# One core, two transformer blocks in float32: order of the products in a step, first squares, forget logits, key sums and norm sums

## The chip, the core and the metric

The kernel runs on one of the eight cores of a Trainium2 chip. A core has TensorE for matrix products (PE, its weight loads are listed as PEld), VectorE (DVE), ScalarE (ACT), GpSimd (POOL) and SyncE (SP), which mainly issues transfers; all work side by side and wait for each other by semaphores. TensorE reads SBUF and adds up in PSUM. The metric is the device time of one execution in microseconds (us). A profile records one execution; its span runs from the first to the last instruction.

## The reference

Two blocks follow each other on x, 256 positions of 2048 channels, all in float32. The first has four branches, the second three, then both have an MLP:

```python
xn = rms_norm(x, norm_mix_g); proj = xn @ w_in          # LRU, pool, short conv, attention, gates
f_logit = proj[..., forget columns]                      # 8 of them, one per head
cum = cumsum(log_sigmoid(f_logit + f_bias))              # enters the first attention's logits
x = x + sum_k(sigmoid(gate_k) * (y_k @ w_branch_k)) @ w_out
x = x + square(relu(rms_norm(x) @ w_mlp_up)) @ w_mlp_down
# second block: gMLP, state-space mixer (s5), stick-breaking attention
z = q @ k.T * scale
log_1m = where(mask, log_sigmoid(-z), 0)
after = cumsum(log_1m, reverse) - log_1m                 # the key sums
w = where(mask, exp(log_sigmoid(z) + after), 0); y = w @ v
return rms_norm(x, final_g)                              # after the second block's own MLP
```

A norm needs the mean of squares over all 2048 channels of a position.

## The kernel before, in words

**Layout.** x stands transposed: `T4[0..3]` are four tiles of 128 channels-in-partitions x 4 x 256 positions. The big products run on float32r, which TensorE takes in one pass, where a float32 product shows up as two passes in the profile. To keep precision, every operand is split in a high part and a rest (`split`, `split_scaled`): ScalarE writes the high part as float32r, VectorE subtracts it and writes the rest. `R[0..7]` hold split activations, high and low side by side, so 512 columns; x itself goes to `xg` = `R[0..3]` multiplied by the norm's gain `gs`, while the norm's factor per position is multiplied in when a product leaves PSUM.

**Steps.** The weights come in units of 1 MB (two steps). The list of products is a list of groups, each of four to eight steps that add up in one of two PSUM buffers `ps`. For each step, ScalarE casts its weights' high part (L145) and VectorE takes the rest (L76, `w<-raw,w`), three steps ahead (`AHEAD`), into one of four buffers `w`; the raw unit's buffer is then free for a later load. In mode "F" (L166 to L170) the weights stay in TensorE and x moves: per step two halves m of the output rows times four k, each a product of the high weights with 512 columns (high and low x) and one of the low weights with 256 columns (high x). In mode "W" the activations stay and the weights move, twelve products of 512 columns.

**Order.** One loop over the steps (`run_stream`) writes everything: it splits the weights of step i + 3, lets finished groups leave PSUM (`late`), writes the products of step i, and then spends a budget of VectorE time on two chains of small work (`chain_a`, `chain_b`: norms, branches, attention, state scan). A chain's `yield None` means: go on in the next step. `need` runs chain_a on at once until a flag is set, where a group depends on it. `hold` keeps a group in PSUM until the norm's factor is there.

**The start.** `first_work` issues the first loads on SP: x's first quarter, the gains, the first unit in two parts, x's second quarter, the second unit, and so on. Steps 0 to 3 also split one quarter of x each (`split_x`), and `squares_x` lets GpSimd square it and add it up in `acc`. `norm` then sums over the channels by products with a column of ones: eight passes of one column on TensorE (x4 in the program, each float32 product two passes), then GpSimd takes the power -0.5, and two products spread the factor over the partitions.

**Forget logits** (`forget`): sixteen products of `wfr` (the eight columns, high and low side by side, 16 wide) with the split x, 512 columns each; then four small products with `sel` add high and low and turn the result.

**Second attention** (`attn2`): per half two rounds of two heads; `e` holds the terms per key, and products with the triangle `tri` and with ones give the sums over keys, in float32 (names `mx<-e,k` and `mx<-e,cst`), six per round. "bu" and "yps" are chain_b's small products: "bu" is a pair of 256 columns on float32r, "yps" eight float32 products into four groups of 32 output rows.

**The end.** The last norm ("n5") sums `acc` and `sq2`, the square of the last group, twelve passes behind the final square; then the output is multiplied by the factor and stored.

## Time and profile before

| | |
|---|---|
| median of 3 runs | 3056.75 us (3053.06 to 3058.41) |
| profiled execution | 3056.62 us, its span 3054.4 us |
| mean granted clock of TensorE | 0.996 of full speed |
| TensorE busy | 3021.8 us (99%), 16127 products (passes counted) |
| weight loads busy | 2576.8 us (84%) |
| VectorE busy | 2061.9 us (68%) |
| ScalarE busy | 1406.2 us (46%) |
| GpSimd busy | 87.9 us (3%) |
| transfers | 604 MB, mean 198 GB/s |

The busy time of a product reaches from its start to its modelled end, so products that follow each other overlap, and the pace is read from starts and counts, not from the busy time. A row of the time order merges like instructions that follow each other; its first number is the start of the first. Names: `w<-raw,w` is the split of weights, `ps<-R,w` a product of mode F, `ps<-w,R` one of mode W, `mx` a small PSUM tile. In a row of a stretch, the counts hold every instruction that touches it, those that reach in from before too.

### The profile page before, as it was taken

Reading aid. Unit: us, or ns where it says so; the run is one execution under the profiler, and the core shown is the slowest. Engines: PE = TensorE matmul, PEld = TensorE weight load, DVE = VectorE, ACT = ScalarE, POOL = GpSimd, SP = SyncE. Lnnn points to the kernel's source line nnn. Section 1 sums busy time; section 2 is a strip of 40 time slices with the busy share of each in tenths; the row PEclk is TensorE's granted clock in tenths of the full one; section 3 lists DMA queues with packets and bytes.
Section 4 is the critical chain, followed back from the end, with each engine's and each line's share of the span. In section 5 each row is a group of like instructions: output and inputs, shape, how many; then the busy total and the mean of one; then the engine's idle time right before and its main releaser. Section 6 shows DMA issues by size and latency. Waiting matters only on the chain.

```text
span 3054.4 us, 39707 instructions
## 1 busy us (share of the span) xinstructions
PE 3021.8 (99%) x16127; PEld 2576.8 (84%) x16127; DVE 2061.9 (68%) x2524; ACT 1406.2 (46%) x1657; POOL 87.9 (3%) x115
## 2 busy tenths in 40 slices
PE   7999999999999999999999999999999999999998
PEld 6888888888888888888888887888888888888887
DVE  6765555556788976566678889966666656565565
ACT  4455544444444434344445564455444434344443
POOL 3000000000000000000010100000000000000000
PEclk9999999999999999999999999999999999999999
DMA  5544455555566665555576666765655555555553
GB/s 211 179 179 163 169 193 193 193 212 188 194 227 215 227 215 199 187 186 193 203 255 215 200 230 219 245 211 199 210 202 184 183 190 183 189 183 189 184 189 124
DMA packets 162071, 603.97 MB, mean 198 GB/s; under 512 B 11568, under 2 KB 13920, under 8 KB 161632
## 3 DMA queue, kind: packets, MB, share of 16 engines
q1 hardware_dynamic: 150528, 569.96, 52.8%
q0 software_dynamic: 7328, 24.12, 2.8%
q10 hardware_dynamic: 4032, 7.34, 0.9%
q8 instruction: 127, 2.08, 0.3%
q14 instruction: 56, 0.46, 0.0%
HBM read 583.53 MB, written 17.85 MB: 197 GB/s over the span
## 4 chain that ended last, share of the span: by engine, by line
PE 74%; issue 24%; DVE 1%; DMA 0%; ACT 0%; SPq 0%; POOLq 0%; POOL 0%; DVEq 0%; ACTq 0%
PE ps L91 72%; PE mx L91 2%; DVE w L76 0%; DVE R L85 0%; PE bu L91 0%; DMA T<-in_x 0%; PE yps L91 0%; PE mx L448 0%; DVE T L76 0%; ACT w L145 0%; PE mx L992 0%; DVE pa L76 0%; PE mx L1115 0%; DVE acc L76 0%; DVE sg L85 0%
## 5 line engine op out<-in xcount | busy, mean ns | idle before, releaser
L91 PE MATMUL ps<-R,w 128*128 128x512 f32 (+1 forms) x11264 | 2002.3, 340 | 17.1 <-ACT w L145 8.8
L91 PEld LDWEIGHTS ps<-R,w 128*128 128x128 f32 x11264 | 1729.7, 189 | 280.4 <-DVE w L76 9.2
L76 DVE TENSOR_TENSOR w<-raw,w 128x1024 fp32r<-128x1024 f32 x1048 | 1282.2, 1224 | 947.0 <-ACT w L145 944.9
L145 ACT CAST w<-raw 128x1024 fp32r<-128x1024 f32 x1048 | 1101.2, 1051 | 1545.3 <-PE ps L91 1375.6
L91 PE MATMUL ps<-w,R 128*128 128x512 f32 x4128 | 951.9, 391 | 0.0
L91 PEld LDWEIGHTS ps<-w,R 128*128 128x128 f32 x4128 | 771.8, 188 | 160.9 <-issue 1.8
L76 DVE TENSOR_TENSOR T<-T,ps 128x512 f32<-128x512 f32 x160 | 109.3, 683 | 9.1 <-PE ps L91 6.3
L76 DVE TENSOR_TENSOR ab<-ps,ab 128x512 f32<-128x512 f32 x98 | 66.9, 683 | 0.0
L332 POOL TENSOR_TENSOR rt<-nv,mh 128x2 f32<-128x2 f32 x5 | 3.5, 706 | 2011.0 <-DVE nv L82 2011.0
L378 ACT COPY ab<-ps 128x512 f32<-128x512 f32 x98 | 56.8, 579 | 0.0
L76 DVE TENSOR_TENSOR R<-ab,R 128x512 fp32r<-128x512 f32 x68 | 46.6, 685 | 0.0
L76 DVE TENSOR_TENSOR ab<-ab,rbc 128x512 f32<-128x512 f32 x64 | 44.3, 692 | 2.2
L96 ACT CAST R<-ab 128x512 fp32r<-128x512 f32 x68 | 41.8, 615 | 5.6 <-DVE ab L76 5.4
L85 DVE SCALAR_TENSOR_TENSOR ab<-ab 128x512 f32<-128x512 f32 x64 | 43.8, 684 | 0.0
L85 DVE SCALAR_TENSOR_TENSOR R<-T,gs,R 128x256 fp32r<-128x256 f32 x64 | 39.1, 657 | 4.3 <-ACT R L88 4.3
L1398 DVE TENSOR_TENSOR_SCAN pb<-magT,pa 128x256 f32<-128x256 f32 x64 | 40.7, 676 | 0.7
L88 ACT ACT_TABLE_LOAD x28 | 35.9, 1283 | 1.2 <-PEq L1528 0.7
L88 ACT ACTIVATE R<-T,gs 128x256 fp32r<-128x256 f32 x64 | 28.5, 498 | 4.9 <-DMA T<-in_x 2.7
L1341 POOL DMA_DIRECT2D tab<-dtab x32 | 17.8, 557 | 248.0 <-DVE pz L76 181.0
L76 DVE TENSOR_TENSOR sg<-ps,sg 128x1024 f32<-128x1024 f32 (+1 forms) x24 | 22.8, 952 | 2.4 <-PE ps L91 2.4
L76 DVE TENSOR_TENSOR pa<-pa,pb 128x256 f32<-128x256 f32 x64 | 24.1, 417 | 0.1
L76 DVE TENSOR_TENSOR T<-T,sg 128x1024 f32<-128x1024 f32 (+1 forms) x24 | 23.0, 958 | 0.8
(229 smaller groups left out, 862.3 us busy)
## 6 DMA issues: line engine op xcount, KB each, us to landing
raw<-in_w_in SPq DMA_DIRECT2D x191, 1024.0 KB, 4.7
raw<-in_w_up SPq DMA_DIRECT2D x128, 1024.0 KB, 4.8
raw<-in_w_down SPq DMA_DIRECT2D x128, 1024.0 KB, 4.8
raw<-in_w_branch SPq DMA_DIRECT2D x40, 1024.0 KB, 4.9
raw<-in_w_out SPq DMA_DIRECT2D x32, 1024.0 KB, 4.7
dtab<-tb SPq DMA_DIRECT2D x16, 512.0 KB, 7.5
tab<-dtab POOLq DMA_DIRECT2D x32, 256.0 KB, 3.9
sg<-dbg ACTq DMA_DIRECT2D x20, 256.0 KB, 4.7
```

The source lines that it names most:

```text
L76: self.V.tensor_tensor(out, a, b, op=op)
L85: self.V.scalar_tensor_tensor(out, a, s, b, op0=op0, op1=op1)
L88: self.A.activation(out, a, func, **kw)
L91: self.T.matmul(out, lhsT, rhs, start=start, stop=stop, skip_group_check=True)
L96: self.A.copy(hi, src)
L145: self.A.copy(hi, raw)
L332: self.G.tensor_tensor(out, v, self.mh[:, 0:out.shape[-1]], op=ALU.pow)
L378: self.A.copy(t, ps[:, :, 1])
L1341: self.G.dma_start(tab[t], self.d_tab[t // 2][:, t % 2])
L1398: self.V.tensor_tensor_scan(b[:, c], mg, a[:, c], 0.0, op0=MUL, op1=ADD)
```

## The change

1. In mode F a step now writes its eight products of 512 columns first and then its eight of 256 (`mm_step`).
2. The start: gains on ScalarE's queue, x's first quarter and the first unit's first step in two parts each, x's second quarter ahead of the first unit's second step; step 0's weights are split in two halves; five float32 products on zeros stand ahead of the first step.
3. The squares of x are taken by ScalarE behind the casts of steps 4 and 5, two each, and VectorE adds them (`sum_squares_x`).
4. `norm` adds the two halves of `acc` on VectorE first (`fold_acc`), so half the products are left; in "n5" seven products of 128 columns on constants stand between those of `acc` and those of `sq2`.
5. `evac_proj` moves a group out of PSUM into its target before the norm's factor is there, and multiplies later.
6. The forget logits use x unsplit in float32, the weights times the gain, 32 wide (24 columns of zeros), into four groups of output rows; `sel` adds the four groups.
7. The second attention's `e` is split in high and low (in `R[0]`, free there), `tri` and ones are copied to float32r, and the key sums take eight float32r products per round and head pair.

```diff
@@ -124,4 +124,6 @@
         if halves:
-            for a in range(2):
-                self.S.dma_start(t[:, a], src[idx + a])
+            for h in range(2):
+                self.S.dma_start(t[:, 0, 512 * h:512 * h + 512], src[idx][:, 512 * h:512 * h + 512])
+            self.S.dma_start(self.T4[1], self.I["x"][1])
+            self.S.dma_start(t[:, 1], src[idx + 1])
         else:
@@ -144,5 +146,10 @@
             hi, lo = w[:, :, 0], w[:, :, 1]
-        self.A.copy(hi, raw)
-        self.tt(lo, raw, hi.bitcast(F32), SUB)
+        for ks in ((slice(0, 2), slice(2, 4)) if i == 0 else (slice(None),)):
+            self.A.copy(hi[:, ks], raw[:, ks])
+            self.tt(lo[:, ks], raw[:, ks], hi[:, ks].bitcast(F32), SUB)
         self.wsp[i] = w
+        if 3 < i < 6:
+            for j in range(2 * i - 8, 2 * i - 6):
+                self.act((self.scr[0], *self.T4[4:7])[j], self.T4[j], AF.Square)
         if slot == 1:
@@ -162,11 +169,13 @@
         w, ps = self.wsp.pop(i), g.ps
-        for m in range(2):
-            ms = slice(128 * m, 128 * m + 128)
-            if g.mode == "F":
-                for k in range(4):
-                    first, last = c == 0 and k == 0, c == g.steps - 1 and k == 3
-                    x = g.movs[c][:, k]
-                    self.mm(ps[:, m], w[:, k, 0, ms], x, first, False)
-                    self.mm(ps[:, m, 0], w[:, k, 1, ms], x[:, 0], False, last)
-            else:
+        ms = [slice(128 * m, 128 * m + 128) for m in range(2)]
+        if g.mode == "F":
+            mk = [(m, k) for m in range(2) for k in range(4)]
+            x = g.movs[c]
+            for m, k in mk:
+                self.mm(ps[:, m], w[:, k, 0, ms[m]], x[:, k], c == 0 and k == 0, False)
+            for m, k in mk:
+                self.mm(ps[:, m, 0], w[:, k, 1, ms[m]], x[:, k, 0], False, c == g.steps - 1 and k == 3)
+        else:
+            for m in range(2):
                 for k in range(2):
...
@@ -278,10 +287,10 @@
         I, S = self.I, self.S
-        S.dma_start(self.T4[0], I["x"][0])
-        S.dma_start(self.gs, I["gs"])
+        self.A.dma_start(self.gs, I["gs"])
+        self.V.memset(self.acc, 0.0)
+        for h in range(2):
+            S.dma_start(self.T4[0][:, 2 * h:2 * h + 2], I["x"][0][:, 2 * h:2 * h + 2])
         self.load_unit(0, halves=True)
-        self.V.memset(self.e32, E32)
-        self.act(self.acc[:, 0, 0:32], self.e32, AF.Copy)
-        S.dma_start(self.T4[1], I["x"][1])
-        self.load_unit(1)
+        self.act(self.rbc[:, 0:32], self.acc[:, 0, 0:32], AF.Copy)
         S.dma_start(self.T4[2], I["x"][2])
+        self.load_unit(1)
         S.dma_start(self.T4[3], I["x"][3])
@@ -289,2 +298,7 @@
         self.load_unit(2)
+        ps = self.mxt("warm")
+        for _ in range(5):
+            self.mm(ps[:, 0:256], self.acc[:, 0, 0:128], self.acc[:, 1])
+        self.V.memset(self.e32, E32)
         self.V.memset(self.mh, -0.5)
@@ -297,14 +311,10 @@
             self.split_scaled(self.xg[j], k, self.T4[j][:, k], self.gs[:, 0, kk:kk + 1])
-        self.squares_x(j)
-    def squares_x(self, j):
-        t = self.sgt("sqx")
-        G = self.G
-        G.tensor_tensor(t, self.T4[j], self.T4[j], op=MUL)
-        if j == 0:
-            G.tensor_tensor(self.acc, t[:, 0:2], t[:, 2:4], op=ADD)
-        else:
-            for h in range(2):
-                G.tensor_tensor(self.acc, self.acc, t[:, 2 * h:2 * h + 2], op=ADD)
+    def sum_squares_x(self):
+        a = self.scr[0]
+        for t in self.T4[4:7]:
+            self.tt(a, a, t, ADD)
+            yield 1.2
+        self.tt(self.acc, a[:, 0:2], a[:, 2:4], ADD)
+        yield 0.7
@@ -330,2 +340,5 @@
+    def fold_acc(self):
+        self.tt(self.acc[:, 0], self.acc[:, 0], self.acc[:, 1], ADD)
     def rsqrt(self, out, v):
@@ -338,9 +351,19 @@
             yield None
+        parts = [self.acc[:, 0]]
+        if tag == "n5":
+            parts += [self.sq2[:, 0], self.sq2[:, 1]]
+        else:
+            self.fold_acc()
+            yield None
         ps = self.mxt()
-        parts = [t[:, a] for t in ([self.acc, self.sq2] if tag == "n5" else [self.acc])
-                 for a in range(2)]
-        for j in range(2):
-            for n, t in enumerate(parts):
+        for n, t in enumerate(parts):
+            for j in range(2):
                 self.mm(ps[:, j:j + 1], t[:, 128 * j:128 * j + 128], self.ones[:, 0:1],
-                        n == 0, n == len(parts) - 1)
+                        n == 0 and j == 0, n == len(parts) - 1)
+            if tag == "n5" and n == 0:
+                w = self.mxt("warm")
+                for _ in range(7):
+                    self.mm(w[:, 0:128], self.ident, self.ones)
         yield None
@@ -383,5 +406,9 @@
         def evac(ps):
-            yield from self.hold(norm)
-            t = self.ab(ps)
-            self.tt(dst(), t, self.bc(), MUL)
+            d = dst()
+            self.A.copy(d, ps[:, :, 1])
+            self.tt(d, ps[:, :, 0], d, ADD)
+            while norm not in self.have:
+                yield 0.0
+            self.tt(d, d, self.bc(), MUL)
             if flag:
@@ -466,2 +493,4 @@
                 self.squares(d, j == 0 and s == 0, j == 3 and s == 1 and flag == "x2e")
+                if j == 3 and s == 0 and flag == "x2e":
+                    self.fold_acc()
                 if flag and j == 3 and s == 1:
@@ -645,3 +674,4 @@
             yield None
-        yield from self.norm("n1", fast=True)
+        yield from self.sum_squares_x()
+        yield from self.norm("n1")
         yield from self.forget()
@@ -725,3 +755,4 @@
             o += w
-        self.wfr = p.tile([128, 16, 2, 8], F32R, name="wfr")
+        self.wf = p.tile([128, 16, 32], F32, name="wf")
+        self.V.memset(self.wf, 0.0)
         for t in self.pad:
@@ -746,14 +777,16 @@
             yield None
-        wf = k["wf"].rearrange("p (k n) -> p k n", k=16)
-        self.A.copy(self.wfr[:, :, 0], wf)
-        self.tt(self.wfr[:, :, 1], wf, self.wfr[:, :, 0].bitcast(F32), SUB)
+        wf = self.wf
+        self.tt(wf[:, :, 0:8], k["wf"].rearrange("p (k n) -> p k n", k=16),
+                self.gs[:, 0].unsqueeze(2).to_broadcast([128, 16, 8]), MUL)
+        yield None
         yield None
         ps = self.mxt()
-        for kt in range(16):
-            self.mm(ps[0:16], self.wfr[:, kt].rearrange("p a b -> p (a b)"),
-                    self.xg[kt // 4][:, kt % 4], kt == 0, kt == 15)
+        for c in range(4):
+            for q in range(4):
+                self.mm(ps[32 * q:32 * q + 32, 0:256], wf[:, 4 * c + q], self.T4[c][:, q],
+                        c == 0, c == 3)
         yield None
         r = self.scr[0].rearrange("p a t -> p (a t)")
-        self.A.copy(r[0:16, 0:512], ps[0:16])
+        self.A.copy(r[:, 0:256], ps[:, 0:256])
         yield 0.1
@@ -762,6 +795,3 @@
         for j in range(2):
-            for i in range(2):
-                n = (16, 8)[i]
-                self.mm(ps[:, 8 * j:8 * j + 8], r[0:n, 256 * i + 128 * j:256 * i + 128 * j + 128],
-                        k["sel"][0:n], i == 0, i == 1)
+            self.mm(ps[:, 8 * j:8 * j + 8], r[:, 128 * j:128 * j + 128], k["sel"])
         yield None
@@ -1175,2 +1205,3 @@
         self.gss = p.tile([128, 8], F32, name="gss")
+        self.tro = p.tile([128, 2, 128], F32R, name="tro")
@@ -1179,3 +1210,6 @@
         v = self.qkv[half][2].rearrange("p (j a) t -> p j (a t)", j=2)
-        mask, tri = self.k2[:, 0:128], self.k2[:, 128:256]
+        mask, (tri, ones) = self.k2[:, 0:128], (self.tro[:, i] for i in range(2))
+        if half == 0:
+            self.A.copy(tri, self.k2[:, 128:256])
+            self.A.copy(ones, self.ones)
         scale = 128.0 ** -0.5
@@ -1211,2 +1245,9 @@
             yield None
+            hl = self.R[0].rearrange("p a b t -> p (a b t)")[:, 0:1536].rearrange(
+                "p (c h n) -> p c h n", c=2, h=2)
+            self.A.copy(hl[:, 0], e)
+            self.tt(hl[:, 1], e, hl[:, 0].bitcast(F32), SUB)
+            yield 0.9
+            yield None
             pss = []
@@ -1214,5 +1255,6 @@
                 ps = self.mxt()
-                self.mm(ps[:, 0:256], tri, e[:, i, 0:256], True, False)
-                self.mm(ps[:, 128:256], self.ones, e[:, i, 256:384], False, True)
-                self.mm(ps[:, 256:384], tri, e[:, i, 256:384])
+                for c in range(2):
+                    self.mm(ps[:, 0:384], tri, hl[:, c, i], c == 0, False)
+                for c in range(2):
+                    self.mm(ps[:, 128:256], ones, hl[:, c, i, 256:384], False, c == 1)
                 pss.append(ps)
```

TensorE, the end of the program (`ps` with 512 or 256 is the last step of mode F, then the last norm), before:

```order
L91 MATMUL ps_23083<-R_81,w_23078 128x512
L91 MATMUL ps_23083<-R_81,w_23078 128x256
L91 MATMUL mx<-cst,acc 128x1 x2
L91 MATMUL mx<-cst,sq_92 128x1 x2
L91 MATMUL mx<-cst,acc 128x1 x2
L91 MATMUL mx<-cst,sq_92 128x1 x2
L91 MATMUL mx<-cst,rt 128x128 x2
```
and now:

```order
L91 MATMUL ps_23070<-R_81,w_23065 128x512 x8
L91 MATMUL ps_23070<-R_81,w_23065 128x256 x8
L91 MATMUL mx<-cst,acc 128x1 x2
L91 MATMUL warm<-cst 128x128 x7
L91 MATMUL mx<-cst,sq_92 128x1 x4
L91 MATMUL mx<-cst,rt 128x128 x2
```
The alternating pairs became two rows of eight; the products of `sq2` (here `sq_92`) now stand last together, and "warm" stands ahead of them.

GpSimd from the start of the program (`sqx` is the square of x, `T_82` to `T_85` are x's quarters), before:

```order
L304 TENSOR_TENSOR sqx<-T_82 128x1024
L306 TENSOR_TENSOR acc<-sqx 128x512
L304 TENSOR_TENSOR sqx<-T_83 128x1024
L309 TENSOR_TENSOR acc<-acc,sqx 128x512 x2
L304 TENSOR_TENSOR sqx<-T_84 128x1024
L309 TENSOR_TENSOR acc<-acc,sqx 128x512 x2
L304 TENSOR_TENSOR sqx<-T_85 128x1024
L309 TENSOR_TENSOR acc<-acc,sqx 128x512 x2
```
and now:

```order
L345 ISA
L345 TENSOR_TENSOR rt<-nv,mh 128x2
L804 TENSOR_TENSOR sm_149<-e_98,sm_149 128x16
L719 TENSOR_TENSOR sm_149<-e_98,sm_149 128x4
L345 TENSOR_TENSOR rq<-sm_149,mh 128x32
```
The squares and their sums are gone; GpSimd's first work is the first norm's power.

ScalarE, from the third split of x on (`R<-T,gs` splits x, CAST is the high part of a step's weights), before:

```order
L88 ACTIVATE R_76<-T_84,gs 128x256 x4
L145 CAST w_184<-raw_112 128x4x256
L88 ACTIVATE R_77<-T_85,gs 128x256 x4
L145 CAST w_199<-raw_112 128x4x256
L145 CAST w_221<-raw_117 128x4x256
L145 CAST w_240<-raw_117 128x4x256
```
and now:

```order
L88 ACTIVATE R_76<-T_84,gs 128x256 x4
L148 CAST w_185<-raw_115 128x4x256
L88 ACTIVATE R_77<-T_85,gs 128x256 x4
L148 CAST w_196<-raw_115 128x4x256
L148 CAST w_218<-raw_119 128x4x256
L88 ACTIVATE scr_135<-T_82 128x1024
L88 ACTIVATE T_86<-T_83 128x1024
L148 CAST w_239<-raw_119 128x4x256
L88 ACTIVATE T_87<-T_84 128x1024
L88 ACTIVATE T_88<-T_85 128x1024
L148 CAST w_262<-raw_175 128x4x256
```
The squares stand behind the casts of steps 4 (`w_218`) and 5 (`w_239`).

## Rows read from the trace of the kernel before

**Rows 1.** The page's first line: span and instructions of the profiled execution
```profile
span 3054.4 us, 39707 instructions
```

**Rows 2.** Groups by shape: engine, operation, count, busy us, mean ns, idle before
```profile
L91 PE MATMUL ps<-R,w 128*128 128x512 f32 x5632 | 1996.3, 399 | 9.1 <-ACT w L145 8.8 <-DVE ab L76 0.3
L91 PEld LDWEIGHTS ps<-R,w 128*128 128x128 f32 x11264 | 1729.7, 189 | 280.4 <-DVE w L76 9.2 <-ACT w L145 8.8 <-PE ps L91 0.6
L91 PE MATMUL ps<-R,w 128*128 128x256 f32 x5632 | 1583.7, 281 | 8.1 <-DVE w L76 8.1
L76 DVE TENSOR_TENSOR w<-raw,w 128x1024 fp32r<-128x1024 f32 x1048 | 1282.2, 1224 | 947.0 <-ACT w L145 944.9
L145 ACT CAST w<-raw 128x1024 fp32r<-128x1024 f32 x1048 | 1101.2, 1051 | 1545.3 <-PE ps L91 1375.6 <-issue 149.2 <-DVE tb L76 5.3
```

**Rows 3.** Stretches of TensorE: length, busy us (products), granted clock, DMA share, GB/s
```profile
112.00:152.00 40.00, 40.00 (x233) 1.00 0.57 197
2100.00:2140.00 40.00, 40.00 (x178) 1.00 0.61 211
2400.00:2600.00 200.00, 200.00 (x1133) 1.00 0.54 185
```

**Rows 4.** TensorE in time order, W products around "bu": start, us, operation
```profile
1917.57 0.40 PE L91 MATMUL bu<-xs,ws 128*128 128x256 f32 x2
1917.80 8.35 PE L91 MATMUL ps<-w,R 128*128 128x512 f32 x36
1925.99 0.40 PE L91 MATMUL bu<-xs,ws 128*128 128x256 f32 x2
```

**Rows 5.** TensorE in time order, W products behind alternating F products
```profile
1659.68 5.67 PE L91 MATMUL ps<-w,R 128*128 128x512 f32 x24
1665.19 1.47 PE L91 MATMUL mx<-z,T 128*128 128x256 f32 x8
```

**Rows 6.** All engines in time order, the first splits of x
```profile
4.41 1.70 ACT L88 ACTIVATE R<-T,gs 128x256 fp32r<-128x256 f32 x4 [2.14 <-DMA gs<-in_gs]
...
10.77 6.56 DVE L85 SCALAR_TENSOR_TENSOR R<-T,gs,R 128x256 fp32r<-128x256 f32 x4 [0.80 <-ACT R L88]
...
26.89 1.66 DVE L85 SCALAR_TENSOR_TENSOR R<-T,gs,R 128x256 fp32r<-128x256 f32 x4
```

**Rows 7.** Stretches of 2 us: PE, PEld, DVE, ACT, POOL, clock, DMA, GB/s
```profile
2.00:4.00 2.00, 0.00 (x0) 0.00 (x0) 0.00 (x0) 0.25 (x2) 0.00 (x0) 1.00 0.82 262
4.00:6.00 2.00, 0.00 (x0) 0.00 (x0) 1.05 (x1) 1.59 (x4) 1.85 (x1) 1.00 0.79 154
6.00:8.00 2.00, 0.00 (x0) 0.00 (x0) 2.00 (x3) 0.45 (x2) 1.36 (x2) 1.00 1.00 408
```

**Rows 8.** All engines in time order: first norm's and forget logits' products
```profile
36.86 0.95 PE L91 MATMUL mx<-cst,acc 128*128 128x1 f32 x8
...
55.60 3.84 PE L91 MATMUL mx<-R,wfr 128*16 128x512 f32 x16
```

**Rows 9.** TensorE in time order, one "yps" block and what follows it
```profile
1908.04 0.40 PE L91 MATMUL yps<-acc,ct 128*32 128x256 f32 x1
...
1909.04 0.51 PE L91 MATMUL bu<-xs,ws 128*128 128x256 f32 x2
```

**Rows 10.** TensorE in time order, one round of key sums and what follows
```profile
1646.40 0.59 PE L91 MATMUL mx<-e,k 128*128 128x256 f32 x2
...
1648.07 0.48 PE L91 MATMUL bu<-xs,ws 128*128 128x256 f32 x2
```

**Rows 11.** All engines in time order, the last norm
```profile
3040.27 0.61 PE L91 MATMUL mx<-cst,sq 128*128 128x1 f32 x4 [1.82 <-ACT sq L88]
...
3041.43 0.99 PE L91 MATMUL mx<-cst,sq 128*128 128x1 f32 x4
...
3043.52 1.23 PE L91 MATMUL mx<-cst,rt 128*128 128x128 f32 x4 [1.10 <-POOL rt L332]
```

**Rows 12.** A stretch of second attention and state scan (columns as in rows 7)
```profile
1800.00:2000.00 200.00, 198.76 (x947) 162.18 (x946) 183.95 (x270) 98.24 (x126) 15.24 (x28) 1.00 0.70 238
```

More of the change, by code (lines that the diff above doesn't have):

```diff
@@ L174, in mm_step @@
                     x = g.movs[c // 2][:, 2 * (c % 2) + k]
-                    self.mm(ps[:, m], x[:, 0, ms], w[:, k, 0], first, False)
-                    self.mm(ps[:, m], x[:, 0, ms], w[:, k, 1], False, False)
-                    self.mm(ps[:, m], x[:, 1, ms], w[:, k, 0], False, last)
+                    self.mm(ps[:, m], x[:, 0, ms[m]], w[:, k, 0], first, False)
+                    self.mm(ps[:, m], x[:, 0, ms[m]], w[:, k, 1], False, False)
+                    self.mm(ps[:, m], x[:, 1, ms[m]], w[:, k, 0], False, last)
         if c == g.steps - 1:
@@ L278, in first_work @@
         I, S = self.I, self.S
-        S.dma_start(self.T4[0], I["x"][0])
-        S.dma_start(self.gs, I["gs"])
+        self.A.dma_start(self.gs, I["gs"])
+        self.V.memset(self.acc, 0.0)
+        for h in range(2):
+            S.dma_start(self.T4[0][:, 2 * h:2 * h + 2], I["x"][0][:, 2 * h:2 * h + 2])
         self.load_unit(0, halves=True)
-        self.V.memset(self.e32, E32)
-        self.act(self.acc[:, 0, 0:32], self.e32, AF.Copy)
-        S.dma_start(self.T4[1], I["x"][1])
+        self.act(self.rbc[:, 0:32], self.acc[:, 0, 0:32], AF.Copy)
+        S.dma_start(self.T4[2], I["x"][2])
         self.load_unit(1)
-        S.dma_start(self.T4[2], I["x"][2])
         S.dma_start(self.T4[3], I["x"][3])
```

## Prediction

> **What bounds the kernel now.** I read the busy shares first: TensorE is busy for 99% of a span of 3054.4 us [rows 1], so what counts is the pace of its products, and not who waits for whom. The profiled execution took 3056.6 us, 2.2 more than its span and 0.1 under the median of the runs shown; the sum below is made against 3056.6. The groups by shape come next: 5632 products of 512 columns and as many of 256, eight and eight in each step of mode "F", so 704 such steps [rows 2]. The stretches give their pace. In 200 us of nothing else 1133 products are counted; less the one or two that reach in over the edge that is 0.1767 us for the mean product, 0.3533 for a pair (512, 256) and 2.827 for a step of eight pairs. The unchanged steps of mode "W" run 512 columns after 512 columns: 178 less two in 40 us, 0.2267 each. From 112 to 152 us the same alternating pairs ran at 0.346 (233 less two) [rows 3]; so a pair has two paces, and neither is the sum of its columns at 2.4 GHz (0.320). The rest of the loss lies at the two ends: the first five steps end at 36.86 us, where the first norm's products stand [rows 8], though five steps cost 14.1.
>
> **The rows of one length (the largest unknown).** After the change a step is eight products of 512 columns and then eight of 256. No stretch of before has a long row of 256-column products on float32r. The nearest is the pair "bu" between W products: it starts at 1917.57, the next product at 1917.80, so 0.115 to 0.12 each [rows 4]. But the products behind pay for it: 36 of them take 8.19 us up to the next pair where 36 times 0.2267 is 8.16, so 0.03 more. Behind an alternating stretch the surcharge is larger: 24 products of 512 columns take 5.51 us instead of 5.44, 0.07 more [rows 5]. Each step of the changed kernel has one such place, where its row of 512 follows a row of 256. So: 8 x 0.117 = 0.936, and 8 x 0.2267 = 1.813 plus a surcharge between 0.03 and 0.07; I take 0.04, because in rows 5 ten products share it and here eight: 2.79. That is 0.037 less than now, and 704 x 0.037 = **26 us**.
>
> Bounds. Below: a row of 256 that takes its columns alone at 2.4 GHz, 0.107 each, and no surcharge gives 2.667, or -113 us; with the 0.12 of half a pair at the better pace (0.346 less 0.2267) and no surcharge 2.773, or -38. Above: counting the surcharge of rows 4 on the pair itself, one "bu" costs 0.115 + 0.015 = 0.13; eight of them and eight of 512 are 2.853, or +18 us. These three are what I keep for the range.
>
> A rule speaks against this part. The Trainium skill ("TensorE: Matmul & The Clock Gate", "Packing small matmuls — row/col tiling") says that a weight load overlaps running products only where it goes to another row group; here all loads fill all rows. By it a step would be sixteen loads and sixteen products one behind the other in either order, and this term would be nothing. The trace disagrees in size: a W product every 0.2267 us leaves 0.013 beside its columns, no room for a load in series. So the rule does not decide here, but the forecast's weak point is the same: whether loads hide behind a product of 256 columns as well as behind 512.
>
> **The first five steps.** Before, GpSimd squares x while VectorE splits it. Four splits of x took VectorE 6.56 us at 10.77 with GpSimd at work, and 1.66 us at 26.89 without [rows 6]. The change takes the squares off GpSimd, loads x and the first weights in smaller pieces, and puts the squares behind the casts of steps 4 and 5 on ScalarE. I lay the new order out by the durations of rows 2 and 6: ScalarE 1.70 for x and 1.05 for a cast, VectorE 1.66 and 1.22. Data come by the rate of rows 7: from 2 us on 0.52, 0.31 and 0.82 MB in two us each, and I let 0.82 go on; so the first 0.5 MB of x and its scales are there by 4.0, the first quarter of the weights by 5.5, x's second part by 7.7, the second megabyte's end by 12.8, x's fourth part by 14.0 and the third megabyte by 17. Then ScalarE is done with x at 5.75 and TensorE starts at 6.4 (now 8.8); step 1 starts at 10.4 (second part of x, then its cast), step 2 at 13.8, step 3 at 16.8, step 4 at 19.6 (ends of casts 10.35, 13.75, 16.75; then TensorE's own 2.8). Step 4 ends at 22.4 against 36.86: **14.5 us**. The squares (four of some 1.05 us on ScalarE) fall between casts that TensorE waits for only three steps later, and their sums on VectorE (three like a split of 1.22, one of half) fall behind the last split of x, where it has one split of 1.22 to do in each step of 2.8. If TensorE runs two of these steps at half pace, as it does the last norm's later passes [rows 11], some 5 us of that go; if VectorE's splits stay as slow as at 10.77, nearly all.
>
> **Smaller terms.** Forget logits: sixteen products of 512 columns, busy for 3.84 us with the last one's end [rows 8], 3.63 by 0.2267 each. Now sixteen float32 products of 256 columns, two passes each, in four column groups. The "yps" products run like that: sixteen passes in 1908.04 to 1909.04, 1.0 us [rows 9]; 32 passes, without the lead-in of the first, are 1.85: -1.8 us. The eight passes behind it become four, by the pace of one-column passes (eight in 0.95 [rows 8]): -0.45. The norms n1 to n4 have four passes instead of eight: 4 x 0.45 = -1.8. Key sums: twelve float32 passes a round, 1646.40 to 1648.07, 1.67 us [rows 10]; now eight float32r products, four of 384 columns (between 0.117 and 0.2267, 0.172) and four of 128 (at most a one-column pass, 0.12, at least half of 0.117): 0.92 to 1.17, four rounds, -2.0 to -3.0: -2.5. Their splitting adds some 1.0 us to VectorE and 0.8 to ScalarE in each round; VectorE is busy for 184 of 200 us there [rows 12], so I cover it with the 16 left, and if that cover fails it costs up to 4 us. Tail: from the last square's arrival twelve norm passes run until 3042.42, 2.15 us, the last ones twice as slow as the first; eight passes at the first pace (four in 0.5) are 1.0; the four behind GpSimd took 1.23 and may take half if the seven extra products hold the clock [rows 11]: -1.1 to -1.7, say -1.4. The pooling is finished later and its four products now stand in a block ahead of step 32; VectorE's part of it stands two splits earlier in its queue, so they find their data: at most 1 us.
>
> Sum: 26 + 14.5 + 1.8 + 0.45 + 1.8 + 2.5 + 1.4 = 48.5. **3056.6 - 48.5 = 3008 us.** What is not the row of one length is 22.5 of it, with bounds of 14 (half clock, no cover) and 27.
>
> **Rivals.**
> 1. *The row of 256 gives back what the row of 512 saves.* Each 256 then costs 0.1267, what the alternating pair leaves beside 0.2267. For it: most pairs keep that pace [rows 3], and the surcharges of rows 4 and 5. Against it: the stretch at 0.346. Time: 3056.6 - 22.5 = 3034; with the 0.13 of "bu" 3052, too near to before to be told from it.
> 2. *The row runs better than half a pair.* Nothing then alternates, and both lengths lose their surcharge: 0.113 for 256, in proportion to the 0.2267, gives 2.72, 75 us, so 2959. For it: "bu" starts as close as 0.115. Against it: the products behind it run slow.
> 3. *The start does not move.* The transfers, not VectorE, set the first five steps. For it: a full 0.82 MB in two us from 6 us on [rows 7]. Against it: four splits of 6.56 between 10 and 26 us. Then only 2.4 us of the start come: 3020.
> 4. *Slower: a row of 256 runs at the weight load's pace.* A load lasts 0.189 us in the records [rows 2]; a product of 256 hides 0.117 of it. Alternating, the product of 512 between two loads catches that up; eight in a row have nothing to. At 0.189 each a step is 3.325, +351 us, 3385 in all. It decides from 0.131 us a product on, where 704 steps eat the 22.5 us. Against it: two "bu" at 0.115, and one-column passes with full loads at 0.12 in a row of eight [rows 8]; for it, only that no row of eight was seen here.
>
> The Trainium skill ("TensorE: Matmul & The Clock Gate", "Back-to-back issue gap") gives N/2.4 + 2.5 ns for a lone product, by which a step were 2.6 us and the kernel some 160 us faster before the other terms. The trace has 0.2267 for 512 columns in a row against 0.216 by that rule, so I give it no case beyond the second rival's lower end.
>
> **How the numbers follow.** Forecast, steps of 2.75 to 2.81: 0.55, times 2980 to 3022. First rival: 0.22. Second: 0.13. Third: 0.07. Fourth: 0.03. A measurement here tells 0.2%, 6 us, from no change. The forecast and the first three rivals are faster by more, but for the first one's upper end (0.04, no change) and 0.01 for several covers failing: faster 0.92, same 0.05, slower 0.03. The range leaves out the lower half of the second rival and the upper end of the first with the fourth: 2968 to 3044.
>
> **What would show it.** In a stretch of pure F steps 200 us hold 16 x 200 / 2.79 = 1147 products and not 1133; 1133 again is the first rival, 1176 the second. ScalarE's casts of a steady F stretch come 2.79 us apart. The first norm's products, now four steps later, stand near 34 us. VectorE's four splits of x take about 1.7 us each time, and GpSimd computes nothing in the first 30 us. The products of the forget logits take about 1.9 us, those of the key sums about 1.05 a round. Wrong above all if the starts of 256-column products in a row are more than 0.122 apart.

## The result, and the profile after

The changed kernel took 3018.29 us (median of four executions, 3018.23 to 3020.0) against 3057.58 of the kernel before in the same series: ratio 0.9875, 95% interval 0.9858 to 0.9892. The forecast was 3008, its range 2968 to 3044. The profiled spans are 3054.4 [rows 1] and:

```profile
span 3016.4 us, 39713 instructions
...
PE 2994.8 (99%) x16127; PEld 2576.1 (85%) x16127; DVE 2060.0 (68%) x2540; ACT 1414.3 (47%) x1667; POOL 70.0 (2%) x104
```

So 38.0 us went, 10.5 fewer than the 48.5 of the sum. Both kernels run the same 1048 steps (704 of mode F, 344 of mode W) in the same order, so I compared when each step starts in the two traces. The difference grows and shrinks in few places:

```
steps        stretch                        gained us   forecast there
0 to 5       the first steps                   +14.6    14.5
5 to 56      first norm, forget, pooling        +1.2    4.6 (2.25, 0.45, 51 rows)
56 to 224    products behind attn1's passes     +1.6    0
224 to 545   F steps, n2, n3                   +10.6    12.8
545 to 616   second attention, 32 F steps       +3.0    3.7 (2.5, 32 rows)
616 to 640   the end of gMLP's small work       -3.8    0
640 to 760   W steps, 8 F steps                 -0.2    0.3
760 to 1047  F steps, n4                        +9.3    11.0
the end      last norm                          +1.8    1.4
```

The stretches of TensorE that answer to [rows 3] (length, busy us and products of PE, PEld, DVE, ACT, POOL, granted clock, DMA share, GB/s):

```profile
112.00:152.00 40.00, 40.00 (x228) 35.17 (x228) 32.56 (x45) 24.81 (x34) 0.00 (x0) 1.00 0.49 170
2100.00:2140.00 40.00, 40.00 (x178) 33.10 (x178) 20.79 (x19) 17.95 (x19) 0.00 (x0) 1.00 0.68 216
2400.00:2600.00 200.00, 200.00 (x1149) 175.96 (x1148) 120.60 (x124) 83.15 (x88) 0.00 (x0) 1.00 0.54 189
```

1149 products in 200 us for 1133; by their starts a step takes 2.794 us for 2.827. W steps are unchanged (178). From 112 to 152 us 228 products stand for 233, but this row is no longer a pure stretch: blocks of four small products begin at 143.0, 146.7 and 150.4. Step by step the pure F steps there take 2.794 us, where those of before took 2.773: here the change lost 20 ns in each.

The start, TensorE in time order (start, us, operation, idle before and what ended it):

```profile
6.53 3.38 PE L91 MATMUL ps<-R,w 128*128 128x512 f32 x16 [0.94 <-ACT w L148]
11.01 3.06 PE L91 MATMUL ps<-R,w 128*128 128x512 f32 x16 [1.09 <-ACT w L148]
14.49 19.95 PE L91 MATMUL ps<-R,w 128*128 128x512 f32 x112 [0.43 <-ACT w L148]
35.49 0.61 PE L91 MATMUL mx<-cst,acc 128*128 128x1 f32 x4 [1.04 <-DVE acc L76]
```

Steps 0 to 2 start within 0.7 us of the 6.4, 10.4 and 13.8 laid out. The last row is a new wait: the first norm's products wait 1.04 us for VectorE. Its queue, first at the splits of x, then at that moment, reads:

```profile
4.44 1.68 DVE L85 SCALAR_TENSOR_TENSOR R<-T,gs,R 128x256 fp32r<-128x256 f32 x4 [1.92 <-ACT R L88]
...
8.85 1.69 DVE L85 SCALAR_TENSOR_TENSOR R<-T,gs,R 128x256 fp32r<-128x256 f32 x4 [0.86 <-ACT R L88]
...
33.28 0.68 DVE L76 TENSOR_TENSOR acc<-scr 128x512 f32<-128x512 f32 x1
33.88 1.22 DVE L76 TENSOR_TENSOR w<-raw,w 128x1024 fp32r<-128x1024 f32 x1
35.02 0.42 DVE L76 TENSOR_TENSOR acc<-acc 128x256 f32<-128x256 f32 x1
```

The splits of x are at 1.68 for four (6.56 at 10.77 before, [rows 6]). The added fold of the sum, 0.42, stands behind a weight split of 1.22.

The loss at gMLP (steps 616 to 640), TensorE, then VectorE, then stretches (columns as above):

```profile
1819.19 11.18 PE L91 MATMUL ps<-w,R 128*128 128x512 f32 x48
1833.36 7.31 PE L91 MATMUL ps<-w,R 128*128 128x512 f32 x24 [2.99 <-ACT sg L88]
```

```profile
1825.72 0.69 DVE L76 TENSOR_TENSOR R<-gm,R 128x512 fp32r<-128x512 f32 x1 [0.69 <-ACT R L96]
1826.33 0.69 DVE L76 TENSOR_TENSOR pa<-pb,tab 128x512 f32<-128x512 f32 x1
...
1830.67 1.22 DVE L76 TENSOR_TENSOR w<-raw,w 128x1024 fp32r<-128x1024 f32 x1
1831.81 1.40 DVE L85 SCALAR_TENSOR_TENSOR sg<-ps,rt,sg 128x512 f32<-128x512 f32 x2
```

```profile
1826.00:1830.00 4.00, 4.00 (x20) 3.28 (x18) 4.00 (x8) 3.49 (x4) 0.56 (x1) 1.00 0.16 55
1830.00:1834.00 4.00, 1.01 (x5) 0.58 (x4) 3.21 (x5) 1.39 (x3) 0.00 (x0) 1.00 0.28 88
1834.00:1838.00 4.00, 4.00 (x12) 3.10 (x11) 3.16 (x5) 1.83 (x3) 0.00 (x0) 0.57 0.47 184
```

The kernel before, TensorE and VectorE at the same work:

```profile
1846.90 13.86 PE L91 MATMUL ps<-w,R 128*128 128x512 f32 x60
```

```profile
1859.97 1.40 DVE L85 SCALAR_TENSOR_TENSOR sg<-ps,rt,sg 128x512 f32<-128x512 f32 x2
```

The gate's values `sg` must leave PSUM before TensorE may go on. In the changed kernel VectorE comes to them only at 1831.81, for it works without a gap from 1825.72 on; in the kernel before it reached them while TensorE still had products to do. TensorE stands for 3 us, and behind that the granted clock is 0.57: twelve products in 4 us, seven of them 427 ns apart, the 1.2 GHz level, another 1.4 us.

### The profile page after: what moved, and what is told of

The parts are those of the page before. It is cut to its first block, busy times and chain, and to the rows that moved or that the text cites. A ratio compares the mean times of both kernels' runs of the same rounds, so it can differ in the third digit from the quotient of the medians.

```text
span 3016.4 us, 39713 instructions
## 1 busy us (share of the span) xinstructions
PE 2994.8 (99%) x16127; PEld 2576.1 (85%) x16127; DVE 2060.0 (68%) x2540; ACT 1414.3 (47%) x1667; POOL 70.0 (2%) x104
## 4 chain that ended last, share of the span: by engine, by line
PE 73%; issue 24%; DVE 2%; ACT 1%; DMA 0%; SPq 0%; POOLq 0%; POOL 0%; DVEq 0%; ACTq 0%
PE ps L91 70%; PE mx L91 1%; DVE w L76 1%; DMA raw<-in_w_in 0%; ACT w L148 0%; PE bu L91 0%; PE yps L91 0%; PE mx L475 0%; DVE T L76 0%; DVE pa L76 0%; DVE sg L85 0%; DVE gm L85 0%; DVE gm L76 0%; PE mx L1022 0%; DVE pb L1440 0%
## 5 line engine op out<-in xcount | busy, mean ns | idle before, releaser
L91 PE MATMUL ps<-R,w 128*128 128x512 f32 (+1 forms) x11264 | 1977.2, 338 | 3.1 <-ACT w L148 2.5
L76 DVE TENSOR_TENSOR w<-raw,w 128x1024 fp32r<-128x1024 f32 (+1 forms) x1049 | 1281.8, 1223 | 913.4 <-ACT w L148 911.6
L148 ACT CAST w<-raw 128x1024 fp32r<-128x1024 f32 (+1 forms) x1049 | 1102.3, 1051 | 1491.5 <-PE ps L91 1328.5
L76 DVE TENSOR_TENSOR ab<-ps,ab 128x512 f32<-128x512 f32 x68 | 46.5, 684 | 0.0
L401 ACT COPY ab<-ps 128x512 f32<-128x512 f32 x68 | 39.4, 580 | 0.0
L85 DVE SCALAR_TENSOR_TENSOR R<-T,gs,R 128x256 fp32r<-128x256 f32 x64 | 27.7, 480 | 2.8 <-ACT R L88 2.8
L1390 ACT CAST xs<-xk 128x256 fp32r<-128x256 f32 x32 | 12.8, 402 | 25.9 <-PE bu L91 22.9
```

The costliest lines, as they stand in the source:

```text
L76: self.V.tensor_tensor(out, a, b, op=op)
L85: self.V.scalar_tensor_tensor(out, a, s, b, op0=op0, op1=op1)
L91: self.T.matmul(out, lhsT, rhs, start=start, stop=stop, skip_group_check=True)
L148: self.A.copy(hi[:, ks], raw[:, ks])
L401: self.A.copy(t, ps[:, :, 1])
L1390: self.A.copy(xs[t], xk[kt][:, q])
```

## The experiments

The diffs are shortened: `hi` stands for a product of 512 columns and `lo` for one of 256, and `...` for lines left out. Where a run has one execution I go by the step-by-step difference to the changed kernel, which agrees to 0.1 us in most stretches that two kernels share.

**In turn again** (the changed kernel without its first part), twice:

```
             for m, k in mk:
                 hi(m, k)
-            for m, k in mk:
                 lo(m, k)
```

> The changed kernel with only the order of the products in a step of mode F put back: 512 columns, 256 columns, eight times in turn. Theory: the new order is worth 33 ns in each of the 704 steps (the pure stretches fell from 2.827 to 2.794 us a step), except where the alternating pairs already ran at 0.346; so the step-by-step comparison shows +33 ns in the pure stretches, none from 112 to 152 us, and the end comes 20 to 23 us later than in the changed kernel, near 3039. Rival: the faster step has another cause in this change (less traffic from GpSimd, other neighbours of the steps); then putting the order back costs under 5 us, near 3020.

3010.91 us (five executions: 3007.08 to 3026.21; ratio 0.9855, 0.9838 to 0.9871): not 20 us later but, by the medians, 7 *earlier*, though the intervals overlap. Theory and rival fall. Two long stretches of the profiled execution, which is the slowest of the five:

```profile
1000.00:1200.00 200.00, 200.00 (x1134) 173.48 (x1133) 152.93 (x205) 84.26 (x91) 0.00 (x0) 1.00 0.63 213
2400.00:2600.00 200.00, 200.00 (x1156) 174.90 (x1155) 121.05 (x124) 83.90 (x89) 0.00 (x0) 1.00 0.55 190
```

The same products run at 2.827 us a step in the one and at 2.773 in the other. Starts of products, ns apart, from the records:

```
in turn, worse pace     512: 241, 256: 120, 236, 113, 233, 117, and again     1060 for three pairs
in turn, better pace    512: 231, 256: 112, 233, 117, and again                693 for two pairs
rows of eight           512: 234 236 228 233 231 226 227 227   256: 113 119 120 120 120 120 120 120
```

In pure stretches a pace holds for hundreds of steps (293 to 514 at 2.827; from 801 to the end at 2.773). It changes only where other products or a wait break the row, and not at each break. So I formed another theory, two paces settled at breaks, and profiled the same kernel a second time:

> The same kernel as the run with products in turn, a second look, for the executions of that one lay between 3007 and 3026 us. Theory (pairs in turn have two paces, and a break settles which): this look has other long stretches at 2.773 and at 2.827 us a step than the first one, where steps 226 to 514 and 762 to 794 ran at 2.827 and all behind step 801 at 2.773; its time is 3026 less 53 ns for every step that changed to the better pace. Rival: the stretches are the same, and the spread lies elsewhere (the clock behind attn1's small products, for one, 3 us).

```profile
1000.00:1200.00 200.00, 200.00 (x1156) 174.90 (x1156) 153.85 (x205) 85.85 (x92) 0.00 (x0) 1.00 0.65 218
2400.00:2600.00 200.00, 200.00 (x1155) 176.37 (x1154) 121.06 (x124) 84.04 (x89) 0.00 (x0) 1.00 0.56 190
```

Now steps 265 to 514 and 762 to 794 have the better pace: 53 ns in each, 15.1 us of the 16.7 between the two spans (the rest is attn1's clock, below). The theory holds: the same program took either pace in the same steps.

**The rows alone** (the kernel before with only the first part):

> The kernel before with only the new order of the products in a step of mode F. Theory: the terms of the change add up, so this alone brings 20 to 23 us, near 3035, with the first five steps as late as before. Rival: the new order needs the rest of the change to be felt (TensorE waits for other engines in so many steps that a shorter row only lengthens the waits): under 10 us, near 3048 or later.

3037.29 us (3032.89 to 3037.68; ratio 0.9938, 0.9923 to 0.9952), by the medians 18.5 less than before. Its profiled execution, the fastest of the four (the others are at 3037), is 23.7 below before: 1.2 of it in the first four steps, 1.6 behind attn1, 0.7 at the end and 20.2 in the F steps, at 33 ns each but for the stretches where before had the better pace (20 ns lost in each). The theory holds, in this kernel: the rows are worth 18 to 20 us here and, by the medians, nothing beside the other parts. A pure stretch:

```profile
1000.00:1200.00 200.00, 200.00 (x1149) 175.94 (x1148) 155.26 (x208) 85.76 (x92) 0.00 (x0) 1.00 0.64 216
```

**Longer and shorter rows:**

```
+            for part in ((hi, lo), (lo, hi))[c % 2]:      # rows of sixteen
+            for m in range(2): hi x 4, lo x 4              # rows of four
```

> The changed kernel, but every second step of mode F takes its row of 256 first and its row of 512 behind it, so that rows of sixteen of one length follow each other and a length changes once a step instead of twice. Theory: a row has a pace of its own (0.2267 us for 512, 0.120 for 256) and each change from 256 back to 512 costs some 28 ns on the 512s behind it (they start 234, 236, 228, 233, 231, 226, 227, 227 ns apart, where a row of only 512 has 226.7) and gives 7 to 8 ns on the first 256s (113, 119). With half the changes a step is 2.794 - (28 - 8) / 2 = 2.784: 10 ns x 704 = 7 us less than the changed kernel, near 3012. Rival: the extra on the first five products of a row belongs to the step (its new stationary weights, the moving tile's first reading), not to the change of length: no difference, 3018.

> The changed kernel with rows of four instead of eight: four of 512, four of 256, twice a step, so two changes back to 512 in a step. Theory (a surcharge per change of length): one more change costs 28 ns less the 8 of the first 256s, a step of 2.81, 14 to 20 ns x 704 = 10 to 14 us more than the changed kernel. Rival (anything but strict alternation has the better pace): 2.794 a step, no difference. Second rival (what counts is that the same half of PSUM is added to by consecutive products): the first 512s of a row would show the extra by which half the product before them wrote.

Rows of sixteen: 3012.76 us (3010.86 to 3014.4; 0.9860, 0.9846 to 0.9875), 10.4 ns a step less than rows of eight, 6.2 us of span. Rows of four: 3027.94, 13 ns a step more (in steps 293 to 354 only 6). The third stretch of [rows 3] for sixteen, then four:

```profile
2400.00:2600.00 200.00, 200.00 (x1152) 176.78 (x1151) 121.02 (x124) 83.69 (x88) 0.00 (x0) 1.00 0.55 188
```

```profile
2400.00:2600.00 200.00, 200.00 (x1142) 174.69 (x1141) 119.83 (x123) 83.42 (x88) 0.00 (x0) 1.00 0.55 186
```

Eight products of 512 at 226.7 and eight of 256 at 120 are 2.773. Above that a step has 33 ns with two returns to 512 (rows of four), 20 with one, 10 with half of one: 17 to 21 ns for each return. The theory holds: half of a return saves what it said, and one more costs 13 ns, just under the 14 to 20. The second rival stays untested: in all three orders a row of 512 begins in the PSUM half that the 256 just before it did not write.

**A pair of 256s in each step:**

```
+            for n, (m, k) in enumerate(mk):
+                a, b = (hi, lo) if n < 5 else (lo, hi)
+                a(m, k); b(m, k)
```

> The changed kernel with the products of a step of mode F in turn again (512, 256), but from the sixth pair on the 256 comes first: each step has one place with two 256s behind each other, and between two steps stand two 512s. What the alternating run had shown: pairs in turn have two paces that hold for hundreds of products, 353.3 ns (512s 241, 236, 233 apart, 256s 120, 113, 117) and 346.7 (231 and 233, 113 and 117); breaks by other products change it, and after the pair of bu (two 256s in a row) every look showed the better one. Theory: two 256s in a row set the better pace; then a pure step takes 2.773 to 2.78 in every stretch, 14 to 21 ns less than the changed kernel's 2.794, and the time is 10 to 15 us less, 3003 to 3008, in every execution. Rival: the pace is settled by where in time a break falls, and each change of neighbours costs as a change of row does: then 2.79 to 2.83, the stretches differ from each other, and the executions too.

3031.68 us (3029.38 to 3032.25; 0.9922, 0.9905 to 0.9938), 2.813 a step in both long stretches. The theory falls: the pair doesn't set the better pace. The rival is right on the step, wrong on the spread.

```profile
2400.00:2600.00 200.00, 200.00 (x1139) 174.11 (x1138) 118.61 (x122) 83.02 (x88) 0.00 (x0) 1.00 0.55 189
```

**The place in PSUM** (but for the first `k` of a group, which keeps its order):

```
+                hi(0, k); lo(1, k); hi(1, k); lo(0, k)
```

> The changed kernel with the products of a step in turn, 512 and 256, but a 256 never adds to the half of PSUM that the 512 just before it added to: the halves of the result alternate. Theory: the two paces of products in turn come from a product that adds where the one before it still adds; then with other halves there is one pace only, 2.773 us a step or better in every stretch and every execution, and the end comes 13 to 15 us before the changed kernel's, near 3004. Rival: where the products add is without influence, and the two paces (2.773 and 2.827 us a step, settled at breaks) remain: long stretches of both kinds or of one, the executions up to 20 us apart, anywhere from 3004 to 3030.

3024.04 us (3020.87 to 3039.23; 0.9911, 0.9880 to 0.9942). The rival is right: both paces again, the better one now first.

```profile
1000.00:1200.00 200.00, 200.00 (x1156) 174.90 (x1155) 153.95 (x205) 86.20 (x94) 0.00 (x0) 1.00 0.65 220
2400.00:2600.00 200.00, 200.00 (x1134) 173.38 (x1133) 118.53 (x121) 81.93 (x88) 0.00 (x0) 1.00 0.55 188
```

**The squares on GpSimd again** (the smaller loads stay):

```
-                self.act((self.scr[0], *self.T4[4:7])[j], self.T4[j], AF.Square)
+        G.tensor_tensor(t, self.T4[j], self.T4[j], op=MUL)
+            G.tensor_tensor(self.acc, t[:, 0:2], t[:, 2:4], op=ADD)
-        yield from self.sum_squares_x()
```

> The changed kernel with the first squares and their sums on GpSimd again, in the place where they were; the smaller loads stay. Theory: GpSimd beside VectorE is what made the splits of x slow (6.56 us against 1.66); then VectorE's splits beside GpSimd take 4 us and more again, step 5, which starts at 23.1, starts 6 to 12 us later, and the end with it, 3024 to 3030. Rival: the first steps waited for the transfers, and the smaller loads brought the gain: step 5 starts within 2 us of 23.1, the end near 3018 to 3020.

Step 5 starts at 33.7 for 23.1, the end comes 10.6 us later (1.6 of it attn1's clock). The theory holds; of the start's 14.6 us GpSimd is 10.6. The other 4 are not separated; the rows alone had brought 1.2 by step 4. VectorE, then GpSimd:

```profile
4.24 6.05 DVE L85 SCALAR_TENSOR_TENSOR R<-T,gs,R 128x256 fp32r<-128x256 f32 x4 [1.72 <-ACT R L88]
...
13.59 6.97 DVE L85 SCALAR_TENSOR_TENSOR R<-T,gs,R 128x256 fp32r<-128x256 f32 x4
```

```profile
4.67 1.89 POOL L313 TENSOR_TENSOR sqx<-T 128x1024 f32<-128x1024 f32 x1 [4.22 <-DMA T<-in_x]
...
20.35 3.56 POOL L318 TENSOR_TENSOR acc<-acc,sqx 128x512 f32<-128x512 f32 x2
```

The Trainium skill ("SBUF — State Buffer", "Who interferes with whom") says that VectorE and GpSimd share one pair of ports as an exclusive lock, and that a VectorE instruction with two inputs in SBUF contends with a GpSimd instruction that reads SBUF. The split has two such inputs, and the trace agrees in direction: one takes 1.5 to 1.7 us beside GpSimd and 0.42 without.

**The products ahead of the first step** left out:

```
-        for _ in range(5):
-            self.mm(ps[:, 0:256], self.acc[:, 0, 0:128], self.acc[:, 1])
```

> The changed kernel without the five products that precede the first step. Theory: they hold the granted clock up while the first data come; without them all sixteen products of step 0 and some of step 1 run at half pace (427 and 213 ns), 2.6 us and more of which the later steps win back what they would have waited for their casts: step 5 starts at 23.5 to 24.5 instead of 23.1, the end within 1.5 us of the changed kernel's, not counting the clock behind attn1. Rival: the transfers alone set steps 1 to 4, so step 5 starts at 23.1 as before and nothing is lost.

Steps 4 and 5 start 0.55 us later (step 5 at 23.7) and step 9 0.2: nothing that counts. The theory's start of step 5 comes out, its reason does not: five products of step 0 stand 427 ns apart, not sixteen, and five of the other runs have four or five such products with the added ones ahead. The end, 1.8 later, is attn1's clock (3.2 later) less 1.6 that gMLP's clock did not lose this time.

**The key sums on float32 again:**

```
-            self.A.copy(hl[:, 0], e)
-            self.tt(hl[:, 1], e, hl[:, 0].bitcast(F32), SUB)
-            yield 0.9
-            yield None
...
-                    self.mm(ps[:, 0:384], tri, hl[:, c, i], c == 0, False)
+                self.mm(ps[:, 0:256], tri, e[:, i, 0:256], True, False)
```

> The changed kernel with the second attention's key sums on float32 again, without the two additional steps of a round. Theory: the parts saved 2.2 us of products from step 552 to 616, but the two steps more in each round brought gMLP's last products behind the point where they are needed, which cost the wait of 3.4 us at 1830.0 and half clock for seven products behind it (1.4 us): so without them steps 552 to 616 lose some 2 us, steps 616 to 640 gain 3.5 to 4, and the sum is 1.5 to 2 us less, near 3016.5. Rival: the wait of gMLP has another cause (it was there in part in the kernel before): steps 616 to 640 gain nothing, and the sum is 2 us more, 3020.5.

Steps 552 to 624 lose 4.4 us and 624 to 664 regain 5.4; the balance from step 80 to the end is 1.6 to the good, as the theory has it. In this execution attn1's clock took 1.6 and the first steps 0.6, so the span is 3017.0. The wait at gMLP is gone:

```profile
1820.80 13.86 PE L91 MATMUL ps<-w,R 128*128 128x512 f32 x60
```

**All remedies together** (the key sums on float32 as above), with rows of sixteen, and in turn:

```
+            if tag == "n1":                  # first norm's products a step later
+                yield None
...
+        yield from self.wait("pool")         # pooling ahead of the forget logits
+        yield from self.pool()
         yield from self.forget()
...
                     self.mm(ps[:, c:c + 2], self.scr[i][...], k["blk"])
-        yield None
+            yield None                       # attn1: in two blocks of sixteen
```

> The changed kernel with what the runs pointed to: rows of sixteen (every second step of mode F begins with its 256s), the key sums on float32 without the two steps more, the pooling's products ahead of the forget logits instead of in a block, the first norm's products one step later, and attn1's 32 passes of two columns cut into two blocks of sixteen in two steps. Theory (the terms add up): 3018.3 less 6.2 for the rows, 1.5 for the key sums, 1.6 for the pooling block, 1.3 for the first norm's wait, and up to 1.6 for the half clock behind attn1's passes that some executions have: 3006 to 3008. Rival: each of these only lets the next wait appear (the forget logits, a step later each, end behind where they are needed): 3011 to 3014. With attn1's passes cut, step 66 has no product at 427 ns; if the clock falls there all the same, their cutting was no remedy.

> The same as the run with rows of sixteen and all the remedies, but the products of a step in turn, 512 and 256, as in the kernel before. Theory (two paces, settled at each break): with the better pace in all long stretches it is 704 x 11 ns = 8 us below its neighbour, near 2999; with the worse one in steps 293 to 514 and 801 to 1047, 469 steps, it is 469 x 43 ns = 20 us less 2 above it, near 3025; the executions spread between the two, and the median lies within 5 us of the neighbour's. Rival: one pace is nearly always taken: all executions within 5 us of each other.

Rows of sixteen: 3010.69 us (3010.15 to 3011.14; 0.9847, 0.9834 to 0.9859), the lowest ratio of all, though its interval overlaps that of rows of sixteen alone. In turn: 3023.99 (3008.09 to 3036.23; 0.9888, 0.9865 to 0.9910), 28 us from end to end, as the two paces would have it; but the median is 13 above its neighbour, not within 5. Of the 16.2 between the two profiled spans 3.7 are no pace: in turn, TensorE waits 2.7 us at 1915.96 for VectorE's `sg`, and seven products behind it come 427 ns apart; with rows of sixteen that wait is not there, and why is not shown. The rival on the first one is nearer: the pooling block and the first norm's wait gave nothing. The pooling's products only move (before had them at steps 23 and 24, the change at 31, about 1.5 us both times), so the 1.6 us I had read at step 31 was no loss; by step 56 all the remedies start within 0.02 us of rows of sixteen alone. The key sums keep 0.8.

Attn1's passes: 32 of two columns in a row, 3.5 us. In seven of the ten profiles of the changed kernel and its variants that have them in one row, and in that of before, six to twelve products of 512 columns behind them came 427 ns apart. In the kernel before with the rows alone none did. The stretch behind them, of before, of the changed kernel, and of the first run in turn:

```profile
226.00:230.00 4.00, 4.00 (x15) 3.15 (x14) 0.72 (x1) 1.05 (x1) 3.58 (x1) 0.71 0.14 57
```

```profile
210.00:214.00 4.00, 4.00 (x19) 3.29 (x18) 1.23 (x1) 1.31 (x2) 3.84 (x1) 1.00 0.19 76
```

```profile
208.00:212.00 4.00, 4.00 (x11) 3.23 (x12) 0.19 (x1) 0.00 (x0) 3.31 (x1) 0.50 0.60 244
```

Cut in two (both of the runs above) there were none in either profile:

```profile
204.55 1.84 PE L91 MATMUL mx<-pk,scr 128*128 128x2 f32 x16
206.25 3.03 PE L91 MATMUL ps<-w,R 128*128 128x512 f32 x12
209.12 1.84 PE L91 MATMUL mx<-pk,scr 128*128 128x2 f32 x16
```

With uncut passes some profiles have none either, so these two don't prove the remedy; the four executions with rows of sixteen lie within 1 us of each other, but so do three of the changed kernel's four.

## Why the prediction was right, and where it was not

*Rows of one length, 26 us: 20.2* (in the run of the rows alone; its pace of 2.79 was right). Three things. A step is 2.794, not 2.790: 256 columns take 0.120 instead of 0.117, and the return costs 0.020 net instead of 0.04 on the 512s. That is 3 us. Then the sum multiplied by all 704 steps, though [rows 3] had shown a stretch with the better pace; those steps lost, 3 us more. The step that failed in substance is the comparison itself. I took the pair's 0.3533 as the price of turns and 0.346 as an exception. Both are paces of turns, and before had the worse one in all its long stretches. All its executions on record lie between 3052 and 3060 us, too close together for a long stretch of the better one; why it always gets the worse one is not known. In the second profile of the kernel in turn most F steps took the better one: those behind step 224 gain 30.5 us on before, where those of the changed kernel, with the rows, gain 20.6 (the small terms of three norms in both). So the 26 us price a pace that the kernel with the other parts can also leave without any rows. The first rival (256s at 0.1267) and the fourth (0.189) are out; so is the second (0.113): the first 256 of a row takes 0.113, the next ones 0.120. The third (the start does not move) is out by the 14.6 below; that its 3020 is nearer to 3018 than the forecast is chance.

The Trainium skill ("TensorE: Matmul & The Clock Gate", "Back-to-back issue gap") has a formula by which lone products of 512 and 256 would take, as an estimate, 215.8 and 109.2 ns. The rows show 226.7 and 120, about 11 ns more on both.

*The first five steps, 14.5: 14.6 at step 5*, by the cause named, with the orders of the start as laid out. But this flatters the forecast: of before's time up to step 5 0.8 are the first norm's products, which now stand in step 8. By the forecast's own marks step 4 ends at 23.1 (22.4 laid out) for 36.86, which is 13.8. Then 1.6 went at step 8: 1.04 is the wait, the rest the norm's products there. They were forecast near 34 and came at 35.49, for the fold stands behind a weight split on VectorE. I had counted the sums as hidden, and not the queue ahead of the last one.

*Forget logits, norms.* The forget products stand from 64.50 to 66.37, 1.87 us (forecast 1.85 and "about 1.9"); their step, 18, takes 4.75, 1.95 more than a pure one. *The pooling block* cost nothing. *The end*: forecast 1.4, 1.8 came.

```profile
3004.00 1.05 PE L91 MATMUL mx<-cst,sq 128*128 128x1 f32 x8 [0.16 <-ACT sq L88]
...
3006.15 0.71 PE L91 MATMUL mx<-cst,rt 128*128 128x128 f32 x4 [1.10 <-POOL rt L345]
```

Against [rows 11] the eight passes take 1.05, where the sum had 1.0, and the last four 0.71 instead of 1.23.

*Key sums, 2.5.* A round takes 1.09 (forecast 1.05):

```profile
1624.18 1.25 PE L91 MATMUL mx<-R,tro 128*128 128x384 f32 x8
1625.27 0.45 PE L91 MATMUL bu<-xs,ws 128*128 128x256 f32 x2
```

By step 616 3.0 us had come; without the float32r sums 2.6 of them are gone. But the cover failed: "if that cover fails it costs up to 4 us", and it cost 3.8. Not by an average that ran over (VectorE 184 of 200 us in [rows 12], 177 in the changed kernel): in the one place where gMLP's last work, pushed later by the rounds' longer chain, falls into the same 6 us of VectorE's queue as the gate's evacuation. The half clock behind the wait is 1.4 of it. That the new key sums cause it is shown by their removal; whether the splitting or the two additional steps do was not separated.

*Not in the sum*: 1.6 us behind attn1, where the profiled execution of before fell to the lower clock level and that of the change did not. This is luck: the run of the rows alone, a variant of before, did not fall, and in seven profiles of the changed kernel's variants it did.

What stays open: what decides at a break which pace products in turn take. Neither the PSUM half nor a pair of 256s decides it. Behind the breaks at steps 224 and 704 every profile in turn had the worse one; behind those of the norms the same program took either.

## What to carry to other kernels

A comparison of two orders holds only for the state in which each ran: see in several long stretches, and in several executions, whether the old order has one pace, before its mean is taken as a price. An order with a sure pace (here rows of sixteen, 4 us between executions) can be worth more than one that is at best 10 ns a step faster and at worst 43 slower. And a cover is not a share of 200 us: look at what the covering engine has in its queue in the few microseconds ahead of each evacuation that TensorE waits for.

## What the hardware showed that was not expected

Products of 512 and 256 columns in turn have two paces, 353.3 and 346.7 ns a pair, that hold over hundreds of pairs. Taken in rows, each return from 256 to 512 costs 17 to 21 ns net, spread over the next five products. In a row of 256s the products start 0.120 us apart, though a load of weights, one for each, lasts 0.19 us in the records. And 3.5 us of passes of two columns can be followed by up to twelve products at half the clock, in some executions and not in others.
